# Softmax times values, 96 heads on one core: GpSimd rounds and spreads the values from fp32, and the last head's loads and the last store are split

## The chip, the cores and the metric

One core of a Trainium2 chip. The metric is the device time of one execution in microseconds (us); a median of several executions is quoted with its range. The span is the stretch that the trace covers.

## The reference

```python
scores: (8, 12, 1024, 1024) fp32;  v: (8, 12, 1024, 64) fp32     # 96 heads
attn = exp(scores - max(scores, -1)); attn = attn / (sum(attn, -1) + 1e-8)
out = attn @ v                                                   # fp32
```

## The kernel before

A loop of 24 turns takes four heads each. Scores come in by DMA (4 MB a head); ScalarE (ACT) exponentiates two rows of tiles at a time to fp16; TensorE (PE) transposes them; VectorE (DVE) copies the transposed row from PSUM to `pt`; TensorE multiplies by the values and a column of ones, which gives the row sums; VectorE divides. Here `P = 128`, `R = C = 8` rows and columns of tiles, `D = 64`, `AHEAD = 4` heads a turn, `LAG = 2`, `T = 2`. All transfers are issued by SyncE in a fixed order. A helper, `queue`, keeps that order.

The values of four heads arrive in one load into `v_sb` (fp32). GpSimd (POOL) casts them to fp16 in one instruction, and VectorE spreads them over `vones`, one 32x512 copy behind every second row of heads 0 to 2 and four at the start of a turn:

```python
def cast_v():
    nc.gpsimd.tensor_copy(out=v_half[:], in_=v_sb[:])
def spread_v(k, s, behind=None):
    copy = nc.vector.tensor_copy(out=vones_bufs[k][s*Q:(s+1)*Q, :, 0:D]...,
                                 in_=v_half[k*Q:(k+1)*Q, :, s])
    if behind is not None: after(copy, behind)        # keeps the order of two instructions
...
# in heads(n0), for head k and row r, after the transposes:
    copy = nc.vector.tensor_copy(out=pt[:], in_=psT[:])
    if k < AHEAD - 1 and r % (R // S) == 0:
        spread_v(k + 1, r // (R // S), copy)
...
# finish(): the matmuls of a row that is LAG rows behind, then
    if k % 2 == 1:
        if g == G - 1: normalise(k, st, b, b + 1)     # odd head: after each bank of four rows
    elif r == R - 1:   normalise(k, st, 0, R // G)    # even head: once
```

The end of a turn has three forms; the last two serve the end of the program:

```python
with tc.If(n0 < BH - 2 * AHEAD) as cmp:
    load(AHEAD-2, ...); load_v(...); load(AHEAD-1, ...); store(n0, AHEAD - T)
... # last turn but one
    load(AHEAD - 2, BH - 2, (4, 4))
    load(AHEAD - 1, BH - 1, (4,))
    store(n0, AHEAD - T)
    load(AHEAD - 1, BH - 1, (2, 1, 1), 4)
... # last turn
    store(n0, AHEAD - T)                              # the very last store, 512 KB
```

The softmax here doesn't subtract the row's maximum and nothing guards it: scores larger than these inputs give would overflow.

## Time and profile before

| | before |
|---|---|
| time, median of 3 (range) | 1065.75 us (1065.68 to 1065.76) |
| span of the profiled execution | 1064.0 us |
| moved by DMA | 453.00 MB, 426 GB/s over the span (the page's 434 is HBM traffic, 461.38 MB) |
| mean granted clock | 0.850 |

A time that DMA bounds has digits of 9 in the DMA row of the 40 slices; what is not DMA is in the last slices, and there the chain of waits and each engine's own order of time say what set the end. Those lines are quoted in the prediction. One more of the page matters, from its list of DMA issues (KB each, then the median us from issue to landing): the load of the values waited long in the queue, so its issue had time to spare.

```profile
v_sb<-in_v_dram SPq DMA_DIRECT2D x24, 1024.0 KB, 33.1
```

### The profile page before, as it was taken

How to read it: one execution, taken by the hardware profiler on the slowest of the kernel's cores; microseconds unless marked ns; L12 is line 12 of the kernel's file. 1: busy time of each engine (PE TensorE's matmuls, PEld its weight loads, DVE VectorE, ACT ScalarE, POOL GpSimd, SP SyncE). 2: the span in 40 equal slices, each digit the busy share in tenths (PEclk: the TensorE clock that was granted, in tenths of full speed). 3: DMA queues.
4: the chain of work that ended last, by engine and by line, in shares of the span. 5: the costliest groups of instructions: out<-in, count | busy, mean ns of one | idle time of the engine just before them, and what ended most of it. 6: DMA issues, size and time to landing. Idle time of an engine off the chain costs nothing.

```text
span 1064.0 us, 32161 instructions
## 1 busy us (share of the span) xinstructions
PE 731.4 (69%) x12288; PEld 678.4 (64%) x12288; DVE 786.6 (74%) x1589; ACT 735.6 (69%) x432; POOL 48.1 (5%) x31
## 2 busy tenths in 40 slices
PE   2766766767766677677686776867666777666676
PEld 2665756667666667666575665767565666666675
DVE  3776876868768777677786776868768687687777
ACT  3766776666767668586676866667766668676685
POOL 0000000000000000000000000000000000000000
PEclk9888888878889888888988888888889788898989
DMA  9999999999999999999999999999999999999995
GB/s 397 431 418 434 426 433 434 433 434 432 432 434 432 425 443 430 429 431 428 433 431 436 432 434 434 431 434 424 441 427 434 432 426 435 432 432 428 440 425 236
DMA packets 24772, 453.06 MB, mean 426 GB/s; under 512 B 2752, under 2 KB 2752, under 8 KB 9152
## 3 DMA queue, kind: packets, MB, share of 16 engines
q1 hardware_dynamic: 24768, 453.00, 99.2%
q8 instruction: 4, 0.07, 0.0%
HBM read 436.21 MB, written 25.17 MB: 434 GB/s over the span
## 4 chain that ended last, share of the span: by engine, by line
DMA 81%; ACT 12%; issue 3%; ACTq 1%; PE 1%; DVE 0%; SPq 0%; PEld 0%; DVEq 0%
DMA s_nat<-in_scores_dram 81%; ACT p_nat L255 12%; PE psT L267 1%; ACTq L255 1%; ACTq L226 0%; ACTq L292 0%; PE psO L145 0%; DVE pt L273 0%; PE psO_whole L145 0%; SPq L184 0%; PEld L267 0%; ACTq L320 0%; DVE out_sb L129 0%; SPq L196 0%; PEld L145 0%
## 5 line engine op out<-in xcount | busy, mean ns | idle before, releaser
L255 ACT ACTIVATE p_nat<-s_nat 128x2048 f16<-128x2048 f32 (+1 forms) x408 | 704.8, 1799 | 228.1 <-DMA s_nat<-in_scores_dram 202.2
L267 PE MATMUL psT<-order,p_nat 128*128 128x128 f16 x6144 | 574.9, 246 | 269.9 <-ACT p_nat L255 263.9
L273 DVE COPY pt<-psT 128x1024 f16<-128x1024 f16 x768 | 515.8, 687 | 200.6 <-PE L267 109.4
L267 PEld LDWEIGHTS <-p_nat 128*128 128x128 f16 x6144 | 446.5, 123 | 298.3 <-ACT p_nat L255 295.7
L145 PEld LDWEIGHTS <-pt 128*128 128x128 f16 x6144 | 302.9, 107 | 81.0 <-DVE pt L273 77.7
L145 PE MATMUL psO<-vones,pt 128*128 128x65 f16 x3072 | 177.4, 201 | 53.9 <-DVE pt L273 50.2
L145 PE MATMUL psO_whole<-vones,pt 128*128 128x65 f16 x3072 | 189.9, 211 | 2.7 <-DVE pt L273 2.4
L207 DVE COPY vones<-v_half 32x512 f16<-32x512 f16 x384 | 109.4, 285 | 22.8 <-POOL v_half L203 6.0
L255 ACT ACT_TABLE_LOAD x24 | 30.8, 1283 | 89.8 <-DMA s_nat<-in_scores_dram 81.7
L203 POOL CAST v_half<-v_sb 128x2048 f16<-128x2048 f32 x25 | 47.4, 1896 | 1002.3 <-DVE vones L207 957.1
L129 DVE TENSOR_TENSOR out_sb<-psO,recip 64x256 f32<-64x256 f32 x192 | 81.1, 423 | 6.1
L129 DVE TENSOR_TENSOR out_sb<-psO_whole,recip 64x512 f32<-64x512 f32 x96 | 66.1, 688 | 3.0
L124 DVE RECIPROCAL recip<-psO 128x4 f32<-128x4 f32 x96 | 17.1, 178 | 34.4 <-PE psO L145 17.6
L124 DVE RECIPROCAL recip<-psO_whole 128x8 f32<-128x8 f32 x48 | 9.7, 203 | 4.5 <-PE psT L267 3.9
L71 DVE MEMSET vones<- 128x16 f16 x4 | 0.2, 72 | 0.8 <-PEq L309 0.8
L62 DVE CAST order<-ident 128x128 f16<-128x128 f32 x1 | 0.2, 227 | 0.4 <-POOL ident masks.py:199 0.4
masks.py:199 POOL TENSOR_SCALAR_AFFINE_SELECT ident<-ident 128x128 f32<-128x128 f32 x1 | 0.3, 295 | 0.1
masks.py:197 POOL MEMSET ident<- 128x128 f32 x1 | 0.2, 205 | 0.3 <-POOLq L309 0.3
L309 POOL MEMSET const-float32-0.0<- 128x1 f32 x1 | 0.1, 100 | 0.2 <-issue 0.2
L309 POOL MEMSET const-bfloat16-1.0<- 128x1 bf16 x1 | 0.1, 103 | 0.0
L309 POOL MEMSET const-uint8-127<- 128x1 uint8 x1 | 0.1, 103 | 0.0
L309 POOL MEMSET const-float32-1.0<- 128x1 f32 x1 | 0.1, 100 | 0.0
## 6 DMA issues: line engine op xcount, KB each, us to landing
s_nat<-in_scores_dram SPq DMA_DIRECT2D x96, 4096.0 KB, 35.8
v_sb<-in_v_dram SPq DMA_DIRECT2D x24, 1024.0 KB, 33.1
out_dram<-out_sb SPq DMA_DIRECT2D x48, 512.0 KB, 26.9
s_nat<-in_scores_dram SPq DMA_DIRECT2D x3, 2048.0 KB, 32.4
s_nat<-in_scores_dram SPq DMA_DIRECT2D x1, 1024.0 KB, 25.4
s_nat<-in_scores_dram SPq DMA_DIRECT2D x2, 512.0 KB
```

The costliest lines, as they stand in the source:

```text
L62: nc.vector.tensor_copy(out=order16[:].rearrange("p (t j) -> p t j", t=T), in_=ident32[:].rearrange("p (j t) -> p t j", t=T),)
L71: nc.vector.memset(vo[:, :, D : D + 2], 1.0)
L124: nc.vector.reciprocal(out=recip, in_=psO[:, :, :, D : D + 1])
L129: nc.vector.tensor_tensor(out=rows.rearrange("j (b g) d -> j b g d", g=G), in0=psO[part, :, :, 0:D], in1=recip[part].to_broadcast([W, last ...
L145: nc.tensor.matmul(out=bank[:, g * M : (g + 1) * M], lhsT=pt[:, c * P : (c + 1) * P], rhs=st["vones"][:, c, 0:M], start=(c == 0), stop=(c ...
L203: nc.gpsimd.tensor_copy(out=v_half[:], in_=v_sb[:])
L207: copy = nc.vector.tensor_copy(out=vones_bufs[k][s * Q : (s + 1) * Q, :, 0:D].rearrange("i (h l) d -> i h l d", l=L), in_=v_half[k * Q : ( ...
L255: nc.scalar.activation(out=p_nat[:, g : g + rows, :].rearrange("p r (x v) -> p x r v", v=Q * L), in_=s_bufs[k][:, r + g : r + g + rows, :] ...
L267: nc.tensor.transpose(out=psT[:, c * P : (c + 1) * P], in_=p_row[:, c // L, c % L, :], identity=order16[:],)
L273: copy = nc.vector.tensor_copy(out=pt[:], in_=psT[:])
L309: nc = _bacc.Bacc("TRN2", target_bir_lowering=False, num_devices=1)
```

## The change

Its intent: take the spreading off VectorE, which is busy in the last two heads, and shorten the tail. GpSimd reads the fp32 values and writes rounded fp16 straight into `vones[k]`, in four copies behind the last row of head k; `v_half` and the separate cast go. The last head's scores come in five parts of 2, 2, 2, 1, 1 rows in place of 4, 2, 1, 1, with the store of the turn before standing after the first of them. The last store goes in two halves, split by columns, so that the first half needs only the first of the two closing multiplies.

```diff
-        if r == R - 1 and k == T - 1:
-            store(n0, 0)
-    def store(n0, k):
+        if r == R - 1:
+            spread_v(k)
+            if k == T - 1: store(n0, 0)
+    def store(n0, k, parts=1):            # the same DMA, for parts of the columns
...
-    def cast_v():
-        nc.gpsimd.tensor_copy(out=v_half[:], in_=v_sb[:])
-    def spread_v(k, s, behind=None):
-        copy = nc.vector.tensor_copy(out=vones_bufs[k][s*Q:(s+1)*Q, :, 0:D]..., in_=v_half[k*Q:(k+1)*Q, :, s])
+    def spread_v(k):
+        for s in range(S):
+            nc.gpsimd.tensor_copy(out=vones_bufs[k][s*Q:(s+1)*Q, :, 0:D]..., in_=v_sb[k*Q:(k+1)*Q, :, s])
...
-                load(AHEAD - 1, BH - 1, (4,))
+                load(AHEAD - 1, BH - 1, (2,))
                 store(n0, AHEAD - T)
-                load(AHEAD - 1, BH - 1, (2, 1, 1), 4)
+                load(AHEAD - 1, BH - 1, (2, 2, 1, 1), 2)
...
-                store(n0, AHEAD - T)
+                store(n0, AHEAD - T, T)
...
-                copy = nc.vector.tensor_copy(out=pt[:], in_=psT[:])
-                if k < AHEAD - 1 and r % (R // S) == 0:
-                    spread_v(k + 1, r // (R // S), copy)
+                nc.vector.tensor_copy(out=pt[:], in_=psT[:])
```

More of the change, by code (lines that the diff above doesn't have):

```diff
@@ L80 @@
     v_sb = sb_pool.tile([P, C // L, S, L, D], FP32, name="v_sb")
-    v_half = sb_pool.tile([P, C // L, S, L, D], FP16, name="v_half")
     p_bufs = buffers(sb_pool, 8, [P, EB, SK], FP16, "p_nat")
@@ L156, in finish @@
             normalise(k, st, 0, R // G)
-        if r == R - 1 and k == T - 1:
-            store(n0, 0)
-    def store(n0, k):
-        rows = out_bh.rearrange("(m x) y -> m x y", x=P)
-        dma = nc.sync.dma_start(
-            out=rows[bass.ds((n0 + k) // T, 1)].rearrange("o x y -> (o x) y"),
-            in_=out_bufs[k // T][:].rearrange("x t r d -> x (t r d)"),
-        )
-        for other in stores:
-            apart(dma, other)
-            apart(other, dma)
-        apart(dma, dma)
-        stores.append(dma)
-        queue(dma)
+        if r == R - 1:
+            spread_v(k)
+            if k == T - 1:
+                store(n0, 0)
+    def store(n0, k, parts=1):
+        rows = out_bh.rearrange("(m x) y -> m x y", x=P)
+        size = T * R * D // parts
+        for part in range(0, T * R * D, size):
+            dma = nc.sync.dma_start(
+                out=rows[bass.ds((n0 + k) // T, 1)].rearrange("o x y -> (o x) y")[
+                    :, part : part + size
+                ],
+                in_=out_bufs[k // T][:].rearrange("x t r d -> x (t r d)")[:, part : part + size],
+            )
+            for other in stores:
+                apart(dma, other)
+                apart(other, dma)
+            apart(dma, dma)
+            stores.append(dma)
+            queue(dma)
     stores = []
@@ L200, in load_v @@
         )
-    def cast_v():
-        nc.gpsimd.tensor_copy(out=v_half[:], in_=v_sb[:])
-    def spread_v(k, s, behind=None):
-        copy = nc.vector.tensor_copy(
-            out=vones_bufs[k][s * Q : (s + 1) * Q, :, 0:D].rearrange(
-                "i (h l) d -> i h l d", l=L
-            ),
-            in_=v_half[k * Q : (k + 1) * Q, :, s],
-        )
-        if behind is not None:
-            after(copy, behind)
+    def spread_v(k):
+        for s in range(S):
+            nc.gpsimd.tensor_copy(
+                out=vones_bufs[k][s * Q : (s + 1) * Q, :, 0:D].rearrange(
+                    "i (h l) d -> i h l d", l=L
+                ),
+                in_=v_sb[k * Q : (k + 1) * Q, :, s],
+            )
     def load_next(k, n0):
@@ L235, in last @@
                 load(AHEAD - 2, BH - 2, (4, 4))
-                load(AHEAD - 1, BH - 1, (4,))
+                load(AHEAD - 1, BH - 1, (2,))
                 store(n0, AHEAD - T)
-                load(AHEAD - 1, BH - 1, (2, 1, 1), 4)
+                load(AHEAD - 1, BH - 1, (2, 2, 1, 1), 2)
             with cmp2.Else():
                 queued[:] = before
-                store(n0, AHEAD - T)
+                store(n0, AHEAD - T, T)
     def heads(n0):
         for k in range(AHEAD):
-            if k == 0:
-                for s in range(S):
-                    spread_v(k, s)
             st = dict(vones=vones_bufs[k])
@@ L282, in heads @@
             finish(pending.pop(0))
-        cast_v()
         last(n0)
@@ L289 @@
         load(k, k)
-    cast_v()
+    for k in range(AHEAD):
+        spread_v(k)
     load_v(AHEAD)
```

## The prediction

> **What bounds the kernel now.** I read the page first, its slices and its queue part, because they say whether any engine can matter in the middle of the run. In the first fence the row of DMA digits and the row under it are the 40 slices of the span.
>
> ```profile
> PE 731.4 (69%) x12288; PEld 678.4 (64%) x12288; DVE 786.6 (74%) x1589; ACT 735.6 (69%) x432; POOL 48.1 (5%) x31
> ...
> DMA  9999999999999999999999999999999999999995
> GB/s 397 431 418 434 426 433 434 433 434 432 432 434 432 425 443 430 429 431 428 433 431 436 432 434 434 431 434 424 441 427 434 432 426 435 432 432 428 440 425 236
> ...
> q1 hardware_dynamic: 24768, 453.00, 99.2%
> ...
> L207 DVE COPY vones<-v_half 32x512 f16<-32x512 f16 x384 | 109.4, 285 | 22.8 <-POOL v_half L203 6.0
> ...
> L203 POOL CAST v_half<-v_sb 128x2048 f16<-128x2048 f32 x25 | 47.4, 1896 | 1002.3 <-DVE vones L207 957.1
> ```
>
> Only the last slice of DMA is not full, and the one queue used has its 16 engines busy for 99.2% of the span. No compute engine is over 74%. So 38 slices are worth 453.00 MB over some 434 GB/s = 1044 us, whatever the engines do, and the change removes no byte. The two lower lines are what the change touches: 109.4 us of DVE and 47.4 us of POOL, both beside the stream.
>
> Then the stages of the end, because there the digit falls to 5. A row is the stretch, its length, and the busy us of PE, PEld, DVE, ACT and POOL, then the granted clock, DMA's share and GB/s.
>
> ```profile
> 1030.00:1045.00 15.00, 12.56 (x247) 11.19 (x246) 13.95 (x29) 14.64 (x8) 0.00 (x0) 1.00 1.01 430
> 1045.00:1054.00 9.00, 7.03 (x141) 6.29 (x139) 8.66 (x17) 7.54 (x5) 1.90 (x1) 1.00 0.59 246
> 1054.00:1064.00 10.00, 2.37 (x48) 1.84 (x48) 4.31 (x10) 0.00 (x0) 0.00 (x0) 0.77 0.20 81
> ```
>
> From 1030 to 1054 DVE is busy 22.6 of 24 us and ACT 22.2: in the last two heads the data are there and the two engines set the pace together. Last, the chain that ended last (start, length, what), and DVE's own order of time beside it.
>
> ```profile
> 1013.46 32.39 DMA s_nat<-in_scores_dram
> ...
> 1045.96 1.92 ACT p_nat L255
> ...
> 1049.75 1.91 ACT p_nat L255
> ...
> 1056.69 0.70 DVE pt L273
> ...
> 1058.10 0.19 DVE recip L124
> ```
>
> ```profile
> 1051.76 1.41 DVE L129 TENSOR_TENSOR out_sb<-psO_whole,recip 64x512 f32<-64x512 f32 x2
> 1053.20 1.89 DVE L273 COPY pt<-psT 128x1024 f16<-128x1024 f16 x3
> ...
> 1055.78 0.88 DVE L129 TENSOR_TENSOR out_sb<-psO,recip 64x256 f32<-64x256 f32 x2
> 1056.69 0.69 DVE L273 COPY pt<-psT 128x1024 f16<-128x1024 f16 x1
> 1058.10 0.18 DVE L124 RECIPROCAL recip<-psO 128x4 f32<-128x4 f32 x1 [0.72 <-PE psO L145]
> 1058.31 0.88 DVE L129 TENSOR_TENSOR out_sb<-psO,recip 64x256 f32<-64x256 f32 x2
> ```
>
> The trace's landing events complete it: the five last load parts land at 1041.0 (head 2's second half), 1045.86 (head 3, rows 0 to 3), 1049.63 (rows 4 and 5), 1050.84 and 1052.05 (one row each), a store between the first two of head 3. ACT works without a gap from 1045.96 for 7.59 us, to 1053.55. DVE is behind it: the three copies from 1053.20 are rows 3 to 5, whose exponentials were done between 1049.7 and 1051.7. DVE ends at 1059.19, the final store is issued at 1059.22, moves its first packet at 1060.08 and lands at 1062.15, and 1.83 us later the span ends. Measured time is 1.75 us above the span.
>
> **What the Trainium skill says.** The page "SBUF — State Buffer", section "Who interferes with whom", says that VectorE copies between two SBUF tiles can enter a two-port mode in which they exclude GpSimd, while an operation with a PSUM source does not contend. After the change all DVE work of the loop reads PSUM, so neither engine should hold the other. The trace of before shows no such stall either (the casts take 1891 to 1897 ns). "GPSIMD Engine Reference", section "Engine selection", calls one-input work roughly line-rate; the cast agrees, 2048 elements in 1896 ns. "DMA: Bandwidth & Descriptors", section "Anatomy of one DMA — SWDGE (gpsimd) path", puts some 2 us of fixed time on a transfer, mostly the receipt (for GpSimd's queue; here it is the hardware one); the last store took 2.93 us for 512 KB, of which its packets took 1.4 us, so the trace agrees roughly. The same page's Specifications put the line-rate limit at 512 B; halves make packets of 2 KB.
>
> **The change, part by part.**
> *Spread on GpSimd.* It removes 384 DVE copies of 285 ns (109.4 us) and 25 casts (47.4 us), and adds 16 copies of 32x512 before the loop and 16 in each of 24 turns, 400 in all. An estimate for one, from the cast: 512 of 2048 elements is a quarter of 1896 ns, 474 ns, plus a fixed part, say 0.62 us; 400 x 0.62 = 248 us of POOL, 23% of the span, beside the stream. In the first 37 slices the gain is nil, as DMA is full. What can lose there is the issue of transfers. The load of the next values now waits for the spread of head 3, which waits for that head's last matmul. In the turn whose score load was issued at 99.95, that value load was issued at 93.11; head 3's last normalise ends at 106.89, its matmuls about a us before. Four copies (2.5 us) put the issue at about 108, the score load and the store just behind. The queue is then filled to 123.8, when the load ahead of it lands, so some 15 us of lead remain. Cost: 0.
>
> *DVE at the end.* In head 3 there are no copies of values; they fell in heads 1 and 2 before it. From 1030 on the DVE order of time has nine of them, 9 x 0.31 = 2.8 us. Without them DVE's work for a pair of heads is 16 copies of 0.67, and 3.7 us of normalising with its reciprocals, 14.4 us, against ACT's 14.7: it keeps up with ACT. So the end is followed from ACT:
> - Head 2's exponentials end at 1044.82 as before. Rows 0 and 1 of head 3 have landed by 1043.4 (half of a 4.85 us transfer after 1041.0), so they run to 1046.7. The store and the next part bring rows 2 and 3 at 1047.2, done at 1049.2. Rows 4 and 5 land at 1049.63 as before, and run from 1049.75 as before; row 6 ends at 1052.63, row 7 at 1053.55. So the finer parts start ACT 1.1 us earlier and end it at the same time: worth 0 at ACT's end.
> - DVE now has rows 0 to 3 and head 2's normalise (1.41 us) behind it at about 1051.9. Row 4: transposes from 1051.7, copy 1052.35 to 1053.0. Row 5: copy to 1054.0. In the built order follow bank 0's reciprocal (to 1054.2), row 6's copy (to 1054.9), bank 0's two multiplies of 0.44 (to 1055.84), row 7's copy (to 1056.56), 0.7 us of matmul, reciprocal 0.18 and two multiplies 0.88: end at 1058.36 against 1059.19. Gain 0.83 us.
>
> *The store in halves.* The first half needs the first multiply alone and goes out at 1057.95, the second at 1058.40. With 0.86 us to the first packet its half of 1.4 us of packets runs from about 1059.5, behind the first half: landing 0.7 us sooner than a whole store issued then. Gain 0.7.
>
> The sum is 0.83 + 0.7 = 1.5 us: 1065.75 - 1.5 = 1064.25, rounded to 1064.3.
>
> **The rivals.**
> *The queue runs dry.* For it speaks that SyncE already waits for POOL here (total us, times, longest):
>
> ```profile
> SPq L196 <- POOL v_half L203: 97.3, 23, 5.6
> ```
>
> Those 97.3 us cost nothing, as the slices are full. Each GpSimd copy would have to take over 4 us for the lead of 15 us to go. If it went, every us would be paid in 22 turns: 2 us make 1110.
> *A late engine.* From 70 us on, 4 of the 16 DMA engines land each load 2.1 us after the other 12 (1041.0 against 1038.9). The lag grows where instruction fetches of 16 KB take single engines (27.0, 36.7 and 47.2 us) and around 64 us. Another program may fetch at other places: 1.5 us either way, 1062.8 to 1065.8. The three equal timings of before speak for a lag that repeats.
> *DVE was not what held the end.* Then only the store gains, or not even that if two completions cost what one does: 1065.0 to 1065.8.
> *More than thought.* If bank 0's multiplies did not stand in front of row 7's copy, the path from ACT's end is 0.7 + 0.7 + 0.7 + 1.1 = 3.2 us, and DVE ends at 1056.8: 1062.7.
>
> **Range and chances.** The middle rivals move the time by 1 to 1.5 us either way, the first is held off by its margin. I give 1063.0 to 1065.7 for 8 in 10. A gain over 2% would need 21 us off a full DMA stream (0.3%); a loss over 2% needs the queue dry in most turns (1.2%).
>
> **What would show it.** Right: slices of DMA still 9 to the last, POOL near 250 us without lengthening DVE's 687 ns copies, DVE near 680 us, ACT's last activation ending near 1053.6, DVE's last near 1058.4, two stores of 256 KB whose second lands 2.3 us after its issue. Wrong: DMA digits under 9 in the middle or loads that land soon after issue (queue dry); GpSimd copies over 1 us; an ACT end that has moved by the lag of the four engines, which would then be the larger term.

## The result, and the profile after

| | before | after |
|---|---|---|
| time, median of 4 (range) | 1065.74 us (1065.68 to 1065.76) | 1064.53 us (1064.27 to 1064.83) |
| span of the profiled execution | 1063.98 | 1062.53 |
| spans of the other executions | 1063.6 to 1064.3 in all later sessions | 1062.5 to 1062.8 |

The ratio is 0.9989, with a 95% interval of 0.9972 to 1.0006. Here and below a ratio is the mean time of one kernel's fast runs over that of the other's in the same rounds, so not quite the ratio of the medians quoted. The kernel is the same within 2%. The interval holds 1, so the times alone do not prove a gain, but no span of after reaches the lowest of before.

The page of the changed kernel, with the lines that answer to those of before:

```profile
PE 722.2 (68%) x12288; PEld 679.8 (64%) x12288; DVE 682.4 (64%) x1205; ACT 735.7 (69%) x432; POOL 243.5 (23%) x406
...
DMA  9999999999999999999999999999999999999996
...
q1 hardware_dynamic: 25056, 453.00, 99.3%
...
L271 DVE COPY pt<-psT 128x1024 f16<-128x1024 f16 x768 | 519.5, 690 | 348.4 <-PE L144 126.7
...
L210 POOL CAST vones<-v_sb 32x512 f16<-32x512 f32 x400 | 242.8, 607 | 815.9 <-PE L265 315.9
...
v_sb<-in_v_dram SPq DMA_DIRECT2D x24, 1024.0 KB, 18.4
...
out_dram<-out_sb SPq DMA_DIRECT2D x2, 256.0 KB, 2.0
```

The stream is as full as it was. VectorE lost 104 us and the time did not notice until the last slice, where a 5 became a 6 because the span now ends sooner after the last load. The last line is the store in halves. The value load now lands 18.4 us after its issue in place of 33.1: its issue is later, and its place in the queue is not. The queue's own waits show the same from the other side (total us, times, longest): SyncE now stands 429 us for GpSimd, and none of it reaches the DMA engines.

```profile
SPq L201 <- POOL vones L210: 429.3, 23, 20.0
```

The same three stages of the end as in the prediction (busy us of PE, PEld, DVE, ACT, POOL, then clock, DMA share and GB/s):

```profile
1030.00:1045.00 15.00, 11.87 (x240) 10.79 (x236) 13.20 (x25) 14.88 (x9) 3.62 (x6) 1.00 1.01 427
1045.00:1054.00 9.00, 7.36 (x157) 7.02 (x158) 7.83 (x14) 7.29 (x5) 3.66 (x7) 1.00 0.65 270
1054.00:1064.00 10.00, 1.47 (x31) 1.10 (x28) 3.38 (x9) 0.00 (x0) 2.44 (x4) 0.72 0.17 64
```

From 1030 to 1054 VectorE is busy 21.0 us in place of 22.6, ACT 22.2 as before: more of VectorE's work is done when ACT ends. VectorE's order of time at the end (start, length, what; a trailing xN joins N neighbours):

```profile
1050.10 1.41 DVE L128 TENSOR_TENSOR out_sb<-psO_whole,recip 64x512 f32<-64x512 f32 x2
1051.54 2.48 DVE L271 COPY pt<-psT 128x1024 f16<-128x1024 f16 x4
...
1054.96 0.88 DVE L128 TENSOR_TENSOR out_sb<-psO,recip 64x256 f32<-64x256 f32 x2
1055.87 0.69 DVE L271 COPY pt<-psT 128x1024 f16<-128x1024 f16 x1
...
1057.49 0.88 DVE L128 TENSOR_TENSOR out_sb<-psO,recip 64x256 f32<-64x256 f32 x2
```

Head 2's multiplies start at 1050.10, behind row 1's copy; before they started at 1051.76, behind row 2's. VectorE ends at 1058.37 in place of 1059.19.

The chain of waits of the changed kernel, its last part:

```profile
1049.66 1.91 ACT p_nat L253
...
1055.87 0.70 DVE pt L271
...
1057.42 0.59 POOL vones L210
...
1059.41 0.61 POOL vones L210
```

This is a chain to read with care. It ends on GpSimd, with spreads of head 3's values that no later turn uses. The last of them ends at 1060.02, but the second half of the store lands at 1060.67, after it. So the spreads do not set the end, although the page's shares now list POOL.

The span shrank by 1.45 us: VectorE's end by 0.82 (1059.19 to 1058.37), the stretch from it to the last landing by 0.66 (2.96 to 2.30), and from landing to the end of the span nothing (1.83, 1.86).

### The profile page after: what moved, and what is told of

Its sections match the earlier page's. It is cut to its first block, busy times and chain, and to the rows that moved or that the text cites. A ratio compares the mean times of both kernels' runs of the same rounds, so it can differ in the third digit from the quotient of the medians.

```text
span 1062.5 us, 32878 instructions
## 1 busy us (share of the span) xinstructions
PE 722.2 (68%) x12288; PEld 679.8 (64%) x12288; DVE 682.4 (64%) x1205; ACT 735.7 (69%) x432; POOL 243.5 (23%) x406
## 3 DMA queue, kind: packets, MB, share of 16 engines
q1 hardware_dynamic: 25056, 453.00, 99.3%
## 4 chain that ended last, share of the span: by engine, by line
DMA 61%; PE 15%; PEld 5%; ACT 5%; DVE 4%; issue 3%; POOL 3%; SPq 1%; POOLq 1%; ACTq 0%; PEldq 0%
DMA s_nat<-in_scores_dram 61%; PE psT L265 8%; PE psO L144 6%; ACT p_nat L253 5%; DVE pt L271 4%; PEld L265 3%; POOL vones L210 3%; PEld L144 2%; PE psO_whole L144 2%; SPq L201 1%; SPq L189 0%; POOLq L210 0%; POOLq L227 0%; POOLq L288 0%; POOLq L316 0%
## 5 line engine op out<-in xcount | busy, mean ns | idle before, releaser
L265 PE MATMUL psT<-order,p_nat 128*128 128x128 f16 x6144 | 565.0, 247 | 262.6 <-ACT p_nat L253 261.7
L210 POOL CAST vones<-v_sb 32x512 f16<-32x512 f32 x400 | 242.8, 607 | 815.9 <-PE L265 315.9
L144 PE MATMUL psO<-vones,pt 128*128 128x65 f16 x3072 | 183.2, 202 | 59.9 <-DVE pt L271 59.6
## 6 DMA issues: line engine op xcount, KB each, us to landing
v_sb<-in_v_dram SPq DMA_DIRECT2D x24, 1024.0 KB, 18.4
```

Source lines behind the costliest of these rows:

```text
L144: nc.tensor.matmul(out=bank[:, g * M : (g + 1) * M], lhsT=pt[:, c * P : (c + 1) * P], rhs=st["vones"][:, c, 0:M], start=(c == 0), stop=(c ...
L210: nc.gpsimd.tensor_copy(out=vones_bufs[k][s * Q : (s + 1) * Q, :, 0:D].rearrange("i (h l) d -> i h l d", l=L), in_=v_sb[k * Q : (k + 1) * ...
L265: nc.tensor.transpose(out=psT[:, c * P : (c + 1) * P], in_=p_row[:, c // L, c % L, :], identity=order16[:],)
```

## The experiments

Each was timed in rounds with the kernel before on the same chip. The table gathers their ends from the traces, in us, but for e6, whose end lies 195 us later. "Fetch" is a transfer of 16 KB on the instruction queue. The column says whether one fell beside the last store: there it started 0.4 to 1.0 us before the store's first packet, in the other runs after the store had landed or not at all.

| run | VectorE end | to last landing | store | fetch beside it | median span |
|---|---|---|---|---|---|
| before | 1059.19 | 2.96 | whole | yes | 1063.8 to 1063.9 |
| after | 1058.37 | 2.30 | halves | no | 1062.55 |
| e1, spread only | 1058.48 | 2.64 | whole | no | 1063.4 |
| e2, parts only | 1059.13 | 3.28 | whole | yes | 1064.2 |
| e3, halves only | 1059.37 | 2.29 | halves | no | 1063.4 |
| e4, spread and halves | 1058.45 | 3.03 | halves | yes | 1063.3 |
| e5, 8 adds ahead of the load | 1058.59 | 2.30 | halves | no | 1062.8 |
| e8, earlier store moved | 1058.41 | 3.26 | halves | yes | 1062.5 |
| e9, second half from ACT | 1058.46 | 2.29 | halves | no | 1062.6 |
| e10, bank 0 later | 1058.11 | 3.05 | halves | yes | 1062.3 |
| e11, idle VectorE copies | 1059.36 | 2.32 | halves | no | 1063.5 |
| e12, tiny VectorE copies | 1059.14 | 2.32 | halves | no | 1063.2 |
| e13, row 7 copied by ACT | 1058.51 | 2.29 | halves | no | 1062.7 |

### One part at a time: e1 to e4

The theory: the spread is worth 0.8 us at VectorE's end, the halves 0.7 us behind it, the finer parts nothing. The rivals: the finer parts bring the gain at VectorE's end (e1, e2, e4), or two halves cost what one store costs (e3).

**e1, the spread alone**: the changed kernel with the old parts and one last store.

```diff
-                load(AHEAD - 1, BH - 1, (2,))
+                load(AHEAD - 1, BH - 1, (4,))
-                load(AHEAD - 1, BH - 1, (2, 2, 1, 1), 2)
+                load(AHEAD - 1, BH - 1, (2, 1, 1), 4)
-                store(n0, AHEAD - T, T)
+                store(n0, AHEAD - T)
```

> Spread on GpSimd alone, parts 4,2,1,1 and one last store as before. My theory: DVE was behind ACT at the end, so without its nine value copies its last multiply ends near 1058.5 instead of 1059.19, the store still takes 2.9 us to land; span 1063.3, time 1065.0 (0.7 us under before). Rival (the finer parts carry the gain at the end, GpSimd nothing): span 1064.0, time 1065.7, DVE end near 1059.2.

Measured: 1065.23 us (1064.93 to 1065.42), before 1065.93 beside it, ratio 0.9994 (0.9981 to 1.0008). VectorE ends at 1058.48: 0.71 of the 0.82 us comes with the spread. But the store, still whole, took 2.64 us from VectorE's end, not the 2.96 of before. That was in no theory.

**e2, the finer parts alone**: before, with these loads.

```diff
-                load(AHEAD - 1, BH - 1, (4,))
+                load(AHEAD - 1, BH - 1, (2,))
                 store(n0, AHEAD - T)
-                load(AHEAD - 1, BH - 1, (2, 1, 1), 4)
+                load(AHEAD - 1, BH - 1, (2, 2, 1, 1), 2)
```

> Only the last head's parts 2,2,2,1,1; values still cast on GpSimd and spread by DVE, one last store. My theory: ACT starts head 3 1.1 us earlier but ends at the same 1053.5, and DVE, busy 8.66 of the 9 us before 1054, can't use it: DVE end within 0.3 us of 1059.19, span 1063.7 to 1064.0. Rival (finer parts carry the 0.8 us): span 1063.2, DVE end near 1058.4.

Measured: 1066.03 us (1065.52 to 1066.29), ratio 1.0001 (0.9988 to 1.0015). VectorE ends at 1059.13, 0.06 earlier than before, and ACT at 1053.78. The parts alone are worth nothing.

**e3, the halves alone**: before, with the changed `store` and `store(n0, AHEAD - T, T)` at the end.

> Only the last store in two halves. My theory: DVE end as before at 1059.2, second half lands 2.3 us after it instead of 2.95: span 1063.3, time 1065.1. Rival (two completions cost what one does; the gain in the changed kernel came with DVE alone): span 1064.0, or longer by the second issue of 0.3 us.

Measured: 1065.94 us (1065.29 to 1066.41), ratio 1.0001 (0.9987 to 1.0014). From VectorE's end to the landing it took 2.29 us in place of 2.96, and the median span is 0.4 us shorter, but the median time shows none of it. At this size the times don't decide.

**e4, spread and halves**: the changed kernel with the old parts, so that against it the finer parts are told apart where the spread is there.

> The changed kernel with the parts of the last head put back to 4,2,1,1. My theory: parts are worth little, span 1062.5 to 1062.8, time 1064.3 to 1064.6, as in the changed kernel. Rival (the parts are what lets DVE finish early): span 1063.3, 0.8 us over the changed kernel.

Measured: 1065.05 us (1064.47 to 1065.68), ratio 0.9992 (0.9979 to 1.0006). VectorE's end is 1058.45, so the parts are worth 0.1 us at most. From there to the landing it took 3.03 us, though the store is halved: SyncE's second issue took 1016 ns, where after's took some 330. Its five spans lie on two levels, 1062.5 and 1062.7, and 1063.3 to 1063.9.

What ran beside the store in e1 and e4, but also in before, is a transfer of 16 KB of the instruction queue. In the next fences, each of one kernel's DMA view from 1056 to 1064 us (40 slices of 0.2 us; the q8 line has packets, MB and share), first before, then e1, e4 and after:

```profile
DMA  0000000000000003000069898951000000000000
...
q8 instruction: 1, 0.02, 0.8%
```

```profile
DMA  0000000000000000399999800000000000000400
```

```profile
DMA  0000000000002049970009994000000000000000
GB/s 0 0 0 0 0 0 0 0 0 0 0 0 82 0 195 369 410 277 10 10 20 358 369 451 154 0 0 0 0 0 0 0 0 0 0 0 0 0 0 0
...
q8 instruction: 1, 0.02, 0.7%
```

```profile
DMA  0000000000000099989970000000000040000000
```

The lone digit is the fetch, on a single engine. In before it runs from 1059.06 to 1060.03, so it ends just ahead of the store's first packet (1060.08); the store was issued meanwhile, at 1059.22. In e1 and in after it comes when the store has landed. In e4 it runs from 1058.47 to 1059.35, and the halves have a hole between them, in which single packets pass (10 and 20 GB/s).

A whole store without a fetch takes 2.64 us from VectorE's end (one trace, e1) and halves without one 2.29 to 2.32, so **the halves themselves are worth 0.34 us**. They start 0.46 us sooner, as the first is issued 0.43 us ahead of VectorE's end and e1's store 0.03 behind it, and take 0.12 us longer from that issue to the last landing (2.73 against 2.61).

The other 0.32 of after's gain is that no fetch fell beside its store. Over the kernels of the table, 5 traces of 5 with the fetch beside the store are long (2.96 to 3.28 us) and 8 of 8 without are short (2.29 to 2.64). The landing events of the 16 DMA engines show where the time goes: in before 15 of them had landed their part of the store by 1061.82, 2.63 us behind VectorE's end, and the last one 0.33 us later. In e2 that one is 0.62 us late, and in e4, e8 and e10 it is 0.85 to 1.07 us late with the first half; in the other eight traces the last engine is at most 0.05 us behind. So one late engine makes the long stores. That it is the engine that fetched is not shown, as the trace does not number the engines, and no run moved the fetch alone.

Where the fetch falls is probably not a property of the kernel. The spans of e4 lie on two levels, and of e8's and of e10's five only the profiled one is long (1063.5 against 1062.3 to 1062.6; 1062.9 against 1062.2 to 1062.4). The 0.32 us is then a difference between two traced executions, and not a gain to count on.

### Is the queue's lead as large as thought: e5 and e6

The changed kernel holds the value load until head 3's spread. The prediction said some 15 us of lead remain; the rival is that they don't, or that any delay costs. Both runs put idle GpSimd adds ahead of that load, 8 and then 18:

```diff
             load(AHEAD - 2, (n0 + (2 * AHEAD - 2)) % BH)
+            for _ in range(8):        # e6: 18
+                nc.gpsimd.tensor_tensor(out=spare[:], in0=v_sb[:, :, 0],
+                                        in1=vones_bufs[AHEAD-1][:, :, 0:D]..., op=add)
             load_v((n0 + 2 * AHEAD) % BH)
```

> The changed kernel with 8 spare GpSimd additions (128x512, reading the values and head 3's spread) ahead of each next load of values, in the 22 turns that have one. They hold that load, and behind it the scores of head 3 and a store, by 8 times an estimated 1.2 us, some 10 us. My theory of a lead of 15 us in the DMA queue: no loss, DMA digits 9, time within 0.3 us of the changed kernel (1064.5). Rival (the queue has no such lead): each of 22 turns loses up to 10 us, 1280.

Measured: 1064.83 us (1064.52 to 1065.32), ratio 0.9990 (0.9974 to 1.0005), as after. In the turn that the prediction took, the issue of the value load moved from 108.03 to 117.60 and its landing from 126.181 only to 126.198. The 9.6 us were all absorbed.

> The same with 18 spare additions, a hold of some 22 us, over the lead. My theory: the queue runs dry once a turn; a turn is then 15.8 us from head 3's landing to the spread's end, 22 us of hold and 13.4 us for values and scores of head 3 to land, 51 us instead of 43.7: some 7 to 8 us in each of 22 turns, 1220 to 1245, with DMA digits under 9. Rival (the load's issue does not matter): 1064.5.

Measured: 1259.45 us (1258.14 to 1261.22), ratio 1.1812 (1.1794 to 1.1831), 195 us slower than the changed kernel. The pages of e5 and of e6 (DMA digits; the adds with busy us and mean ns; the value load's us from issue to landing):

```profile
DMA  9999999999999999999999999999999999999996
...
L232 POOL TENSOR_TENSOR spare<-v_sb,vones 128x512 f32<-128x512 f32 x176 | 197.3, 1121 | 14.0
```

```profile
DMA  9989779797797977979789797887979879788797
...
v_sb<-in_v_dram SPq DMA_DIRECT2D x24, 1024.0 KB, 4.8
```

In e6 the queue runs dry in every turn, and a turn takes 53.0 us (from the value load's issue at 188.17 to the next at 241.20) in place of 43.7. So the rival of the dry queue is real, and begins between 9.6 and some 21 us of further delay: it was right to hold it off by a margin of 15 us. The loss was more than the 1220 to 1245 expected, because from the issue until head 3's scores were there it took 15.5 us (188.17 to 203.66), not 13.4; the 18 adds with what goes between them hold 21.6 us, as expected.

### Does an earlier landing or another issuer move the end: e8 and e9

**e8** puts the store of the turn before behind row 5, so that rows 2 to 5 land 1.3 us sooner than in after:

```diff
-                load(AHEAD - 1, BH - 1, (2,))
+                load(AHEAD - 1, BH - 1, (2, 2, 2))
                 store(n0, AHEAD - T)
-                load(AHEAD - 1, BH - 1, (2, 2, 1, 1), 2)
+                load(AHEAD - 1, BH - 1, (1, 1), 6)
```

> The changed kernel with the store of the turn before moved behind the third part of the last head (order 2,2,2,store,1,1). Rows 2 to 5 land 1.25 us earlier, the last two rows as before. If the end hangs on when rows 4 and 5 land and on DVE's order after it, ACT ends near 1053.2 instead of 1053.45 and bank 0's multiplies no longer stand before row 7's copy: DVE end near 1056.7, span 1060.9, time 1062.8. Rival (the end hangs on the last rows' landing, or head 2's normalise now waits for the later store, which lands near 1049.6): span 1062.2 to 1062.8.

Measured: 1064.38 us (1064.07 to 1065.24), ratio 0.9985 (0.9971 to 0.9999). ACT ends at 1053.26, 0.2 earlier, and VectorE at 1058.41, not earlier at all. So an earlier landing of rows 2 to 5 does not move VectorE's end; after row 5's copy the chain of waits goes back and forth between TensorE and VectorE. The profiled store is long (3.26) with the fetch beside it and a second issue of 1257 ns; the other spans, 1062.3 to 1062.6, are like after's.

**e9** is e8 with the second half issued from ACT's queue:

```diff
-            dma = nc.sync.dma_start(
+            dma = (nc.scalar if part else nc.sync).dma_start(
```

> As the run with the later store, and the second half of the last store issued by ACT's queue instead of SyncE's, so that it need not wait for the first half's issue (in the changed kernel the second issue starts 0.25 us after the multiply that it needs). Theory: another 0.2 us, span 0.2 us under that run. Rival: a first transfer on a queue never used before costs more than the issue saves, span equal or longer.

Measured: 1064.54 us (1064.31 to 1064.92), ratio 0.9989 (0.9975 to 1.0002). ACT issued at 1058.49, where SyncE in after did at 1058.62, and it took 2.29 us from VectorE's end to the landing, as after's 2.30. The run does not tell why: ACT's issue was 2.26 us ahead of its landing and SyncE's second 2.05, so the rival, a first transfer on an unused queue that costs what the issue saves, fits as well. The DMA row of after says more. It has no hole between the halves, so the second half's packets follow the first's at once, and an earlier second issue had nothing to gain.

### Is VectorE's time what was gained: e11 and e12

**e11** gives the changed kernel back the 12 copies a turn that VectorE had behind rows of heads 0 to 2, at the same places, writing to a spare tile that nobody reads. GpSimd still spreads.

```diff
-                nc.vector.tensor_copy(out=pt[:], in_=psT[:])
+                copy = nc.vector.tensor_copy(out=pt[:], in_=psT[:])
+                if k < AHEAD - 1 and r % (R // S) == 0:
+                    s = r // (R // S)
+                    idle = nc.vector.tensor_copy(out=spare[s*Q:(s+1)*Q, :, 0:D]...,
+                                                 in_=v_half[(k+1)*Q:(k+2)*Q, :, s])
+                    after(idle, copy)
```

> The changed kernel, values spread by GpSimd, but DVE does 12 copies of 32x512 fp16 a turn to no purpose, in the places where the kernel before spread the values (only the four of head 0 of a turn, which the kernel before did at the turn's start, are left out). TensorE's order of instructions comes out as in the kernel before, instruction for instruction. My theory (DVE's copies, by their time and by the order that they force, held the end): DVE end back near 1059.1, span 1063.2 to 1063.4, 0.8 us over the changed kernel's 1062.5. Rival (the gain came from values being ready earlier): DVE end stays near 1058.4, span 1062.5.

Measured: 1065.58 us (1065.34 to 1066.12), ratio 0.9997 (0.9983 to 1.0011). VectorE ends at 1059.36: the gain is gone. But building it also brought back TensorE's order of before, instruction for instruction, so copies and order moved together. **e12** was made to part them: the same instructions in the same places, with 16 elements a partition in place of 512.

```diff
-                        out=spare[s*Q:(s+1)*Q, :, 0:D]...,   in_=v_half[(k+1)*Q:(k+2)*Q, :, s],
+                        out=spare[s*Q:(s+1)*Q, :, 0:2]...,   in_=v_half[(k+1)*Q:(k+2)*Q, :, s, :, 0:2],
```

> As that, but each idle copy has 16 elements a partition instead of 512, so it costs only the fixed part, some 70 to 150 ns; TensorE's order is then close to the changed kernel's. If DVE's time and the order it forces are the cause, DVE end 1058.4 to 1058.7, span near 1062.6. Rival (the mere number of DVE instructions and waits holds the end): DVE end 1059.1.

Measured: 1064.97 us (1064.87 to 1065.51), ratio 0.9991 (0.9978 to 1.0005). The copies of e11 and of e12 (min, median, max ns, then first and last start):

```profile
L277 DVE COPY spare<-v_half x288: 280/285/599, 21.8 to 1048.9; 32x512 f16<-32x512 f16 x144
```

```profile
L277 DVE COPY spare<-v_half x288: 161/168/568, 21.9 to 1048.2; 32x16 f16<-32x16 f16 x144
```

The spread of these times is the port contention that the prediction set out from: in e11 all 228 copies between SBUF tiles that fell beside no copy of GpSimd took 280 to 291 ns, the 60 beside one up to 599, and VectorE's copies from PSUM took some 690 ns with or without it. The change escapes it because VectorE has no such copies left.

A median copy is 117 ns shorter (168 ns, more than the 70 to 150 expected), and VectorE still ends at 1059.14, against the 1058.4 to 1058.7 that the theory of VectorE's time asked for. In e12's order of time on VectorE head 2's multiplies stand behind row 2's copy again and start within 0.05 us of before's 1051.76:

```profile
1051.71 1.41 DVE L131 TENSOR_TENSOR out_sb<-psO_whole,recip 64x512 f32<-64x512 f32 x2
...
1058.27 0.88 DVE L131 TENSOR_TENSOR out_sb<-psO,recip 64x256 f32<-64x256 f32 x2
```

And in the stretch just before, VectorE was not full: it waited 0.27 and 0.15 us for TensorE. As the trace stands, the time of the copies alone does not explain the 0.82 us. Where the copies stand in the stream, the compiler orders head 2's normalising and TensorE's matmuls differently, and part of the gain seems to go with that order.

How much is not shown. e12's order is near after's on TensorE, not equal to it, and some of its copies took up to 568 ns while GpSimd spread. And its stream ran late in this trace: the last row landed at 1052.39 (1052.02 in after, 1051.98 in e11) and ACT ended at 1053.88 (1053.45, 1053.41). Counted from ACT's end, VectorE ends 5.26 us later in e12, 4.92 in after, 5.64 in before and 5.95 in e11, so the short copies may have won back more than 1059.14 shows. By median spans they won 0.3 of 0.95 us (1063.5 in e11, 1063.2 in e12, 1062.55 in after).

### Is there more to have at the end: e10 and e13

**e10** tries the prediction's last rival: bank 0's multiplies of an odd head go behind row 7's copy. TensorE's order stays that of after but for three matmuls a turn, which move ahead of eight transposes.

```diff
         if k % 2 == 1:
-            if g == G - 1:
-                normalise(k, st, b, b + 1)
+            if r == R - 1 - LAG: normalise(k, st, 0, 1)
+            if r == R - 1:       normalise(k, st, 1, 2)
```

> The changed kernel with the normalise of bank 0 of an odd head put behind the copy of its last row; TensorE's order unchanged. Theory (bank 0's multiplies stand in the way of row 7's copy, and would fit under row 7's matmuls): row 7's copy 0.9 us earlier at 1054.95, DVE end near 1057.8, span 1062.0, time 1063.9. Rival (row 7's copy waits for TensorE anyway): DVE end 1058.4, span 1062.5.

Measured: 1064.31 us (1064.07 to 1064.98), ratio 0.9985 (0.9971 to 0.9998), median span 1062.3. This is the best median, 0.2 us under after's, and with these ranges not to be told from it. Row 7's copy, from VectorE's order of time, with its idle time ahead and what ended it:

```profile
1055.30 0.69 DVE L273 COPY pt<-psT 128x1024 f16<-128x1024 f16 x1 [0.27 <-PE L144]
```

It starts 0.57 us sooner than after's 1055.87, but then waits for TensorE. The multiplies that were moved follow it (1056.11 to 1056.99) and push back bank 1's, so that VectorE's end comes 0.26 us sooner, at 1058.11, not at 1057.8. The rival's 1056.8 left those multiplies out of the sum: moved, they still have to be done before the end.

**e13** is e10 with row 7's copy made by ACT, which is idle by then:

```diff
+                if k == AHEAD - 1 and r == R - 1: nc.scalar.copy(out=pt[:], in_=psT[:])
+                else: nc.vector.tensor_copy(out=pt[:], in_=psT[:])
```

> As the run with bank 0 later, and the last row's copy of head 3 done by ACT, which is idle by then. Theory: the copy and bank 0's normalise run side by side, DVE end near 1057.4, span 1061.6, time 1063.5. Rival (ACT's copy from PSUM is slower by as much as it saves, or ACT's next head waits for it): span 1062.0 or more.

Measured: 1064.81 us (1064.40 to 1065.67), ratio 0.9990 (0.9976 to 1.0004). ACT waited for TensorE until 1055.69 and then took 1.01 us where VectorE takes 0.69; VectorE ends at 1058.51. No gain, and the second half of the rival is in the trace: the copy stands in every turn, and the one of the turn before (1019.83 to 1020.84) held up ACT's next head, whose exponentials began at 1022.34 in place of e10's 1021.62. VectorE was 0.6 us behind e10 from there on (head 2's multiplies at 1050.74 against 1050.13). A copy on ACT in the last turn alone was not tried.

## Why the prediction was right

The time was predicted as 1064.3 and came as 1064.53; of 1.5 us expected, 1.45 showed in the span and 1.21 in the medians. By its steps:

1. **Cost in the stream, 0: right.** (Its 1044 us for 38 slices is a slip: they are 1011 us, and 1044 are 39.) The slices stay at 9 and the 453.00 MB are the same. The value load went out at 108.03 ("about 108"), 15.7 us before the load ahead of it landed at 123.74 ("some 15 us"). e5 took 9.6 us of it at no cost, and e6 shows what the rival would have cost.
2. **GpSimd: right.** A copy took 607 ns (0.62 estimated), the sum 242.8 us (248). VectorE went to 682.4 us ("near 680"), and its PSUM copies from 687 to 690 ns. That the casts of before showed no stall was no test, as none of VectorE's 384 copies fell beside one; e11 is the test.
3. **VectorE's end, 0.83 us: right in size, and its steps from row 5's copy on hit within 0.02 us** (row 5 done at 1054.02, bank 0's multiplies at 1055.84, row 7 at 1056.56, end at 1058.37). e1 shows that the spread brings it. What is not borne out is the reason: the prediction had it come from 2.8 us of VectorE time alone. With short copies and head 2's multiplies still behind row 2, e12's trace stays at 1059.14. In after these multiplies moved ahead of row 2's copy, and at 1051.9 rows 2 and 3 were not yet copied, which the prediction had done by then. How much is order and how much is time stays open.
4. **The halves, 0.7 us: 0.66 measured, but by luck.** 0.34 is the halving (2.64 to 2.30, both without a fetch beside them). The other 0.32 (2.96 to 2.64) came in e1 with the store still whole: it is the one late engine of before's store, 0.33 us behind the other 15. Nor does 0.7 follow from the prediction's own figures. A whole store issued at 1058.40 would send packets from 1059.26 to 1060.66, the second half from 1059.5 to 1060.2, which is 0.46 us sooner. Its 1.4 us of packets is what e1's store took (1.40); before's took 1.65, late engine included. The second issue was at 1058.62, not 1058.40, as SyncE's first took 0.36 us and 0.32 passed between, and its half landed 2.05 us later, not 2.3. That did not limit it, as the halves' packets have no hole between them. Of the fixed time that the prediction took from the Trainium skill as mostly the receipt, before's trace has 0.86 us ahead of the first packet and 0.42 behind the last, so the agreement was in the sum at most.
5. **The finer parts, 0 at ACT's end: right.** ACT ends at 1053.45 (1053.55 before); alone they give 0.06 us at VectorE's end (e2), beside the spread about 0.1.
6. **A late engine: did not come.** Four of the 16 DMA engines are 2.1 us late in both traces (1041.0 against 1038.9 before; 1040.94 against 1038.87 after). The rival's seed was right in another place: a fetch that moved did change the time, at the last store.

So a fair part of the agreement, 0.32 us, is luck: a term that the prediction did not know of, given to one that it did.

## What to carry to other kernels

Where DMA is full in every slice, moving 100 us of work to an idle engine was worth nothing except in the tail, and what must be checked first is how late it makes the next load's issue: here 15.7 us of lead stood against a loss of 195 us. In the tail, taking instructions away also changed the order that the compiler picks; test a gain by putting back cheap instructions in the same places before calling it time saved. Before dividing a last transfer's duration into terms, see what else was on the DMA engines beside it.

## What the Trainium skill lacked or had wrong

- No page says what an instruction fetch does to a store beside it. The fetch is 16 KB on one engine for some 0.9 to 1.2 us; in the 5 traces with it beside the store one of the 16 DMA engines lands its part 0.33 to 1.07 us after the others, in the 8 without at most 0.05. That the fetch causes this is not shown by a run that moves it alone.
- "DMA: Bandwidth & Descriptors", section "Where 436 GB/s comes from", says that between HBM and SBUF the HBM side binds at about 358 GB/s. Here one active core moved 426 GB/s over the span, which fits the 425 GB/s that the same page's table gives for a single core; by the page's note there, 358 is a core's share when both cores of the pair stream.
- "GPSIMD Engine Reference", section "Engine selection", calls one-input work about line-rate and gives no size for what comes on top. A quarter of the large cast (1896 ns) is 474 ns, and the 32x512 copy took 607. Whether the 133 ns are a fixed part or come with the form (32 partitions in place of 128, a spread destination) no run shows.
